# The second layer's modulation vectors are computed in the first layer's output projection and token choice, not with the filters

## The chip, the core and the metric

The kernel runs on one core of a Trainium2 chip. TensorE (PE) multiplies, VectorE (DVE), ScalarE (ACT) and GpSimd (POOL) work on the results, and SyncE (SP) issues most of the DMA transfers. Each engine takes its instructions in a fixed order, decided when the program is built, and an instruction that waits holds all that stand behind it on that engine. The metric is the device time of one execution in microseconds (us); less is better.

## The reference

Two layers work on 1024 latent tokens and 256 context tokens of width 1024. In each layer a modulation of six rows for the latent and six for the context tokens shifts, scales and gates the stream:

```python
mod_l = (jax.nn.silu(c) @ p['mod_w'] + p['mod_b'])[:, None, :]      # mod_w: 1024 x 6144, per layer
mod_c = jax.nn.silu(c_ctx) @ p['mod_w'] + p['mod_b']
hl = modulate(rmsnorm(xl, p['norm1_g']), sh1_l, sc1_l)
ul = hl @ p['w_in']
xl = xl + g1_l * token_mixers(ul, p, cos, sin, keys_l)              # attention, convolution, Hyena; then w_out
hl2 = modulate(rmsnorm(xl, p['norm2_g']), sh2_l, sc2_l)
xl = xl + g2_l * expert_choice_ffn(hl2, p)                          # 16 experts each choose 128 tokens
```

The Hyena part needs long filters that depend on the weights alone. The modulation depends on the two conditioning vectors alone, so the second layer's six rows can be made at any time before that layer starts.

## The kernel before

The program runs through `consts`, `filters` (both layers' Hyena filters and modulation), and then for each layer `win` (first norm and input projection), `mla` (attention, with the convolution and Hyena work beside it), `wout` (output projection, gated residual, router scores, choice of tokens) and `moe` (the experts). A scheduler merges the work of neighbouring stages into one order per engine when the program is built.

**Modulation.** `mod(l, ...)` takes two of the six rows at a time. For each pair it makes eight steps. A step loads 128 x 2048 floats of `mod_w` (1 MB) into a tile `mw`, of which there are three, and multiplies it with the two conditioning vectors `cT`, padded to 32 columns. Four matmuls of 512 columns go to four groups of 32 partitions of one PSUM bank, `macc`. After eight steps DVE adds the bias tile `mb`, scales where a gain `mg` belongs, and SP stores the rows to the DRAM tensor `modd`. The bias loads are issued on ACT's queue. `filters` chains `mod(0)` and `mod(1)` into one list of steps, `steps`, and takes one with `feed(1)` after each piece of filter work.

**Filters.** `spectra` multiplies filter taps (`dh`, `dl`: two parts of each number) with tables `fw` that POOL loads, three matmuls for each product (L95, L96, L97), into banks `p`. DVE and POOL scale the result `gg`, and SP stores it to `gd` or `gdc`.

**Output projection.** In `wout`, `channels(i)` and `heads(i)` handle a tile of 128 tokens: matmuls into banks `mm`, the residual into `xres`, four transposes into each of two banks `tp`, router scores into banks `rt`. `order` lists the ten tiles; tile 7 is the last. Then `route` chooses the tokens: short DVE operations on a tile `ro` with a few small matmuls between them.

**Experts.** `moe` starts with loads of expert 0's weights (four tiles `raw` of 2 MB), and with the matmuls `dt<-rhs,ohc` and `dt<-rhs,oh` that turn the choice into row numbers, by which tokens are gathered.

Of the kernel before, what the change touches and what calls it, by code (L numbers as in the profile page):

```python
# [14 lines left out]
F32 = mybir.dt.float32  # L15
# [4 lines left out]
ALU = mybir.AluOpType  # L20
# [9 lines left out]
def _bc(ap, n):  # L30

    return bass.AP(tensor=ap.tensor, offset=ap.offset, ap=[[0, n]] + [list(x) for x in ap.ap])
# [19 lines left out]
class Kernel:  # L52
# [81 lines left out]
    def mod(self, l, P, ps):  # L134

        nc, A, V = self.nc, self.A, self.V
        w_ = A["mod_w"][l].rearrange("(p k) n -> p k n", k=8)
        for v in range(0, 6, 2):
            acc = ps("macc")
            b = self.t(P, [128, 512], F32, "mb", bufs=1)  # L140
            g = self.t(P, [128, 512], F32, "mg", bufs=1)
# [8 lines left out]
            for k in range(8):  # L150
                w = self.t(P, [128, 2048], F32, "mw", bufs=3)
# [10 lines left out]
                nc.sync.dma_start(self.modd[l][v + j // 2][:, 512 * (j % 2):512 * (j % 2) + 512], b[32 * j:32 * j + 2, :])  # L162
            yield
        self.dump(f"mod{l}", self.modd[l])


    def sin(self, P, out, x, n):
# [180 lines left out]
    def filters(self):  # L348
        A = self.A
        with ExitStack() as es:  # L350
            M = self.pool(es, "mod", 2)
            F = {"f": self.pool(es, "taps", 1), "p": self.pool(es, "sums", 1)}
            ps = self.banks(es, macc=2, p=6)
            steps = chain(self.mod(0, M, ps), self.mod(1, M, ps))

            def feed(n):
                for _ in range(n):
# [10 lines left out]
            with ExitStack() as es2:  # L368
                PL = self.pool(es2, "mlp", 1)
                with ExitStack() as es3:  # L370
                    P = self.pool(es3, "mlps", 1, side="right")
# [669 lines left out]
    def wout(self, l, R):  # L1041
# [4 lines left out]
        with ExitStack() as es:  # L1046
# [6 lines left out]
            else:  # L1053
                PW = self.pool(es, f"wow{l}", 1)
                P = self.pool(es, f"woy{l}", 2)
                PX = self.pool(es, f"wox{l}", 2, side="right")
            ps = self.banks(es, tp=2, mm=4, rt=1, st=1) if last else self.banks(es, tp=2, mm=4, rt=1, st=1)
            gn = self.t(R["pool"], [128, 8], F32, "gn", bufs=1)
            nc.sync.dma_start(gn, A["gn_cols"][l])
            rw = self.t(R["pool"], [128, 8, 32], F32, "rw", bufs=1)  # L1060
# [124 lines left out]
            def router():  # L1185

                n = 1 if last else 2
                rr = self.t(PX, [128, 8, 16], F32, "rr", bufs=1)
                rc = self.t(PX, [128, 2, 2, 8], F32, "rc", bufs=1)
                rs = self.t(PX, [128, 32], F32, "rsum", bufs=1)  # L1190
                nc.sync.dma_start(rr, A["router_w"][l])
                nc.sync.dma_start(sel, A["k_sel"])
                for j, v in enumerate((4, 3)):
                    for s in range(n):
                        nc.sync.dma_start(rc[:, j, s], self.modd[l][v, s].rearrange("(k p) -> p k", p=128))
                if last:
                    G.memset(rw, 0.0)
                    G.memset(rs, 0.0)
                for s in range(n):
                    e = slice(16 * s, 16 * s + 16)  # L1200
                    G.tensor_tensor(rw[:, :, e], rr, rc[:, 0, s].unsqueeze(2).to_broadcast([128, 8, 16]), ALU.mult)
                    tmp = self.t(PX, [128, 8, 16], F32, "rtmp", bufs=1)
                    G.tensor_tensor(tmp, rr, rc[:, 1, s].unsqueeze(2).to_broadcast([128, 8, 16]), ALU.mult)
                    V.tensor_reduce(rs[:, e], tmp.rearrange("p k e -> p e k"), AX.X, ALU.add)
                p = ps("rt")
                self.mm(p[:, 0:32], self.ones[:, 0:1].to_broadcast([128, 128]), rs)
                V.tensor_copy(cst, p[:, 0:32])
# [15 lines left out]
            for n, i in enumerate(order):  # L1223
                end = heads(i)
                if i == 7:
                    self.route(R, ps, "mm" if last else "tp", row() if last else self.t(PX, [128, 1024], F32, "ro", bufs=1))
                    end()
                if n + 2 < nt:
                    channels(order[n + 2])
                if i == 9:  # L1230
                    ar, wk = (self.t(PX, [16, 256], F32, n, bufs=1) for n in ("arc", "wkc"))
                    self.route_ctx(R, ps, ar, wk)
# [595 lines left out]
```

## Time and profile before

| | |
|---|---|
| runs | 3397.47 us median of 3 (3392.35 to 3399.98) |
| profiled execution | 3397.73 us, span 3395.9 us from the first to the last instruction |
| TensorE matmul busy | 3123.1 us, 92% of the span |
| VectorE busy | 2531.3 us, 75% |
| ScalarE busy | 1690.2 us, 50% |
| DMA moved | 660.84 MB, mean 195 GB/s |
| mean granted TensorE clock | 0.954 of full speed |

The busy shares are means over stages with different limits. The span holds the filters up to about 248 us, the first layer's output projection from about 966 us, its choice of tokens up to about 1147 us, and its experts after that. Times in the rows below are microseconds from the start of the span.

### The profile page before, as it was taken

The numbers are of one execution on the slowest core, as the hardware profiler recorded it, in microseconds if no ns is written. First come the engines' busy times: TensorE is split into PE (matmuls) and PEld (weight loads), VectorE is DVE, ScalarE is ACT, GpSimd is POOL, SyncE is SP. The second block draws the span as 40 slices with busy tenths as digits, with TensorE's granted clock in tenths as the row PEclk, the third lists the DMA queues.
The fourth block names the chain that finished last, engine by engine and source line by source line (L and its number), as shares of the span: only waits on it lengthen the run. The fifth ranks groups of instructions, "written<-read, shape, count | busy, mean of one in ns | idle before, by whom it ended". The sixth has DMA issues, their size and how long they took to land. (4 is left out here: it accounts for less than half of the span.)

```text
span 3395.9 us, 42767 instructions
## 1 busy us (share of the span) xinstructions
PE 3123.1 (92%) x15607; PEld 2226.8 (66%) x15607; DVE 2531.3 (75%) x3520; ACT 1690.2 (50%) x2447; POOL 1295.2 (38%) x1128
## 2 busy tenths in 40 slices
PE   8898989999999599999999969899998959999996
PEld 2467865666567376666666657656664747888885
DVE  7755698777657677777777656977775769998986
ACT  4315235433443256656565543353434427777775
POOL 4421255754653212112221122565557423433334
PEclk9898989999999799999999979899999969999998
DMA  8881112231253567777777631221233469999994
GB/s 306 323 279 53 38 64 82 54 104 43 73 162 116 209 241 289 278 286 279 290 292 274 225 101 44 81 72 51 69 110 99 149 235 347 378 382 372 382 378 176
DMA packets 142523, 660.84 MB, mean 195 GB/s; under 512 B 24712, under 2 KB 63272, under 8 KB 111593
## 3 DMA queue, kind: packets, MB, share of 16 engines
q1 hardware_dynamic: 117129, 582.89, 45.6%
q0 software_dynamic: 24768, 74.05, 7.9%
q8 instruction: 123, 2.02, 0.2%
q10 hardware_dynamic: 416, 1.18, 0.1%
q14 instruction: 87, 0.71, 0.1%
HBM read 589.28 MB, written 68.78 MB: 194 GB/s over the span
## 5 line engine op out<-in xcount | busy, mean ns | idle before, releaser
L91 DVE TENSOR_TENSOR mwl<-raw,mwh 128x1024 fp32r<-128x1024 f32 x710 | 881.5, 1278 | 217.5 <-ACT mwh L90 207.2
L90 ACT ACTIVATE mwh<-raw 128x1024 fp32r<-128x1024 f32 x768 | 791.8, 1057 | 350.5 <-PE acc L97 118.1
L96 PE MATMUL acc<-mwl,xh 128*128 128x512 f32 x1024 | 405.0, 396 | 0.0
L97 PE MATMUL acc<-mwh,xl 128*128 128x512 f32 x1024 | 403.0, 396 | 0.1
L95 PE MATMUL acc<-mwh,xh 128*128 128x512 f32 x1024 | 373.7, 401 | 6.0 <-ACT xh L90 6.0
L803 POOL TENSOR_TENSOR psum<-psum,pt 128x512 f32<-128x512 f32 x252 | 332.3, 1338 | 66.7 <-ACT pt L788 56.8
L788 ACT ACTIVATE pt<-s 128x512 f32<-128x512 f32 (+1 forms) x336 | 195.9, 586 | 257.4 <-PE s L97 220.8
L1528 POOL DMA_INDIRECT xd<-ymoe,idx x31 | 113.4, 3656 | 541.6 <-DVE ymoe L1524 465.1
L758 DVE TENSOR_REDUCE mx<-p 128x1 f32<-128x512 f32 (+1 forms) x374 | 206.0, 585 | 70.0 <-PE p L100 68.9
L95 PEld LDWEIGHTS acc<-mwh,xh 128*128 128x128 f32 x1024 | 192.4, 189 | 68.6 <-ACT mwh L90 10.9
L96 PEld LDWEIGHTS acc<-mwl,xh 128*128 128x128 f32 x1024 | 193.9, 189 | 40.1 <-DVE mwl L91 0.8
L91 POOL TENSOR_TENSOR mwl<-raw,mwh 128x1024 fp32r<-128x1024 f32 x58 | 150.1, 2592 | 181.3 <-ACT mwh L90 117.5
L97 PEld LDWEIGHTS acc<-mwh,xl 128*128 128x128 f32 x1024 | 192.8, 189 | 39.1 <-DVE xl L91 0.6
L100 PE MATMUL o<-pt,Vt 128*64 128x512 f32 (+1 forms) x672 | 184.7, 613 | 0.0
L564 DVE SCALAR_TENSOR_TENSOR cacc<-pad,cw,cacc 128x1295 f32<-128x1295 f32 (+1 forms) x90 | 165.8, 1842 | 1.3
L97 PE MATMUL mm<-hTh,wfl 128*128 128x512 f32 (+1 forms) x400 | 151.3, 379 | 12.8 <-DVE wfl L91 12.8
L95 PE MATMUL mm<-hTh,wfh 128*128 128x512 f32 (+1 forms) x400 | 152.5, 381 | 4.0 <-ACT wfh L90 4.0
L96 PE MATMUL mm<-hTl,wfh 128*128 128x512 f32 (+1 forms) x400 | 152.0, 380 | 0.0
L562 POOL TENSOR_TENSOR cacc<-cacc,tap 128x1295 f32<-128x1295 f32 (+1 forms) x30 | 97.0, 3233 | 120.7 <-ACT tap L561 118.5
L100 PE MATMUL cx<-raw,xcT 128*32 128x512 f32 x1024 | 123.7, 607 | 0.0
L95 PE MATMUL mm<-woh,yhh 128*128 128x512 f32 x280 | 115.7, 416 | 8.5 <-ACT wt L1129 4.4
L96 PE MATMUL mm<-wol,yhh 128*128 128x512 f32 x280 | 111.9, 400 | 0.1
(546 smaller groups left out, 7228.9 us busy)
## 6 DMA issues: line engine op xcount, KB each, us to landing
raw<-in_w_gate_dram SPq DMA_DIRECT2D x64, 2048.0 KB
raw<-in_w_up_dram SPq DMA_DIRECT2D x64, 2048.0 KB
raw<-in_w_down_dram SPq DMA_DIRECT2D x64, 2048.0 KB
mw<-in_mod_w_dram SPq DMA_DIRECT2D x48, 1024.0 KB
ht<-in_k_C_dram POOLq DMA_DIRECT2D x24, 512.0 KB, 5.1
wfr<-in_w_fm_dram SPq DMA_DIRECT2D x20, 512.0 KB
hd<-h SPq DMA_DIRECT2D x18, 512.0 KB
fw<-in_k_filt_dram POOLq DMA_DIRECT2D x17, 512.0 KB, 5.8
```

Of the source, the lines that this page charges most:

```text
L90: self.S.activation(hi, src, AF.Copy)
L91: (eng or self.V).tensor_tensor(lo, src, hi.bitcast(F32), ALU.subtract)
L95: mm(out, ah, bh, start=first, stop=False, skip_group_check=True)
L96: mm(out, ah, bl, start=False, stop=False, skip_group_check=True)
L97: return mm(out, al, bh, start=False, stop=last, skip_group_check=True)
L100: return self.T.matmul(out, a, b, start=first, stop=last, skip_group_check=True)
L562: G.tensor_tensor(a, a, t, ALU.add)
L564: V.scalar_tensor_tensor(a, x, w2[:, ct, k:k + 1], a, ALU.mult, ALU.add)
L758: V.tensor_reduce(mx[:, q, n:n + 1], p[:, :N], AX.X, ALU.max)
L788: S.activation(pt[:, :N], p[:, :N], AF.Exp, scale=ATT_SCALE)
L803: (V if tail and n > 8 else G).tensor_tensor(sm[:, :N], st.sums[i][:, :N], pt[:, :N], ALU.add)
L1528: G.indirect_dma_start(self.xd[l], bass.IndirectOffsetOnAxis(ap=d["idx"], axis=0), y, None, compute_op=ALU.add)
```

## The change

`filters` keeps only `mod(0)`. A new function, `mod_row`, makes the second layer's modulation in `wout` of the first layer, one row at a time: six rows of eight steps, 48 steps, each with a load of 128 x 1024 floats (512 KB) into the one tile `mw` and four matmuls of 256 columns. There is one `mb`, one `mg` and one bank `macc`; for that bank `tp` goes from two to one. Four steps are asked for after each tile of tokens, and all that are left after tile 7, behind the choice. The bias and gain loads move from ACT's queue to SP's. `rr` and `rtmp` take the place of the tile `lpart`. The second layer's `wout` makes no steps.

```diff
--- before.py
+++ after.py
@@ -162,6 +162,33 @@
                 nc.sync.dma_start(self.modd[l][v + j // 2][:, 512 * (j % 2):512 * (j % 2) + 512], b[32 * j:32 * j + 2, :])
             yield
         self.dump(f"mod{l}", self.modd[l])
+
+    def mod_row(self, l, P, ps):
+
+        nc, A, V = self.nc, self.A, self.V
+        w_ = A["mod_w"][l].rearrange("(p k) n -> p k n", k=8)
+        for v in range(6):
+            acc = ps("macc")
+            b = self.t(P, [128, 256], F32, "mb", bufs=1)
+            V.memset(b, 0.0)
+            for j in range(4):
+                nc.sync.dma_start(b[32 * j:32 * j + 2, :], _bc(A["mod_b"][l, v * 1024 + 256 * j:v * 1024 + 256 * j + 256], 2))
+            if v in (1, 4):
+                g = self.t(P, [128, 256], F32, "mg", bufs=1)
+                V.memset(g, 0.0)
+                for j in range(4):
+                    nc.sync.dma_start(g[32 * j:32 * j + 2, :], _bc(A["norm1_g" if v == 1 else "norm2_g"][l, 256 * j:256 * j + 256], 2))
+            for k in range(8):
+                w = self.t(P, [128, 1024], F32, "mw", bufs=1)
+                nc.sync.dma_start(w, w_[:, k, v * 1024:v * 1024 + 1024])
+                for j in range(4):
+                    self.mm(acc[32 * j:32 * j + 32, :256], self.cT[:, k, :], w[:, 256 * j:256 * j + 256], k == 0, k == 7)
+                yield
+            V.tensor_tensor(b, acc[:, :256], b, ALU.add)
+            if v in (1, 4):
+                V.scalar_tensor_tensor(b, b, 1.0, g, ALU.add, ALU.mult)
+            for j in range(4):
+                nc.sync.dma_start(self.modd[l][v][:, 256 * j:256 * j + 256], b[32 * j:32 * j + 2, :])
 
 
     def sin(self, P, out, x, n):
@@ -351,7 +378,7 @@
             M = self.pool(es, "mod", 2)
             F = {"f": self.pool(es, "taps", 1), "p": self.pool(es, "sums", 1)}
             ps = self.banks(es, macc=2, p=6)
-            steps = chain(self.mod(0, M, ps), self.mod(1, M, ps))
+            steps = self.mod(0, M, ps)
 
             def feed(n):
                 for _ in range(n):
@@ -1054,7 +1081,13 @@
                 PW = self.pool(es, f"wow{l}", 1)
                 P = self.pool(es, f"woy{l}", 2)
                 PX = self.pool(es, f"wox{l}", 2, side="right")
-            ps = self.banks(es, tp=2, mm=4, rt=1, st=1) if last else self.banks(es, tp=2, mm=4, rt=1, st=1)
+            ps = self.banks(es, tp=2, mm=4, rt=1, st=1) if last else self.banks(es, tp=1, mm=4, rt=1, st=1, macc=1)
+
+            steps = iter(()) if last else self.mod_row(1, self.pool(es, f"mod{l}", 1), ps)
+
+            def feed(n):
+                for _ in range(n):
+                    next(steps, None)
             gn = self.t(R["pool"], [128, 8], F32, "gn", bufs=1)
             nc.sync.dma_start(gn, A["gn_cols"][l])
             rw = self.t(R["pool"], [128, 8, 32], F32, "rw", bufs=1)
@@ -1185,7 +1218,7 @@
             def router():
 
                 n = 1 if last else 2
-                rr = self.t(PX, [128, 8, 16], F32, "rr", bufs=1)
+                rr = self.t(PX, [128, 128], F32, "lpart").rearrange("p (k e) -> p k e", k=8)
                 rc = self.t(PX, [128, 2, 2, 8], F32, "rc", bufs=1)
                 rs = self.t(PX, [128, 32], F32, "rsum", bufs=1)
                 nc.sync.dma_start(rr, A["router_w"][l])
@@ -1199,7 +1232,7 @@
                 for s in range(n):
                     e = slice(16 * s, 16 * s + 16)
                     G.tensor_tensor(rw[:, :, e], rr, rc[:, 0, s].unsqueeze(2).to_broadcast([128, 8, 16]), ALU.mult)
-                    tmp = self.t(PX, [128, 8, 16], F32, "rtmp", bufs=1)
+                    tmp = self.t(PX, [128, 128], F32, "lpart").rearrange("p (k e) -> p k e", k=8)
                     G.tensor_tensor(tmp, rr, rc[:, 1, s].unsqueeze(2).to_broadcast([128, 8, 16]), ALU.mult)
                     V.tensor_reduce(rs[:, e], tmp.rearrange("p k e -> p e k"), AX.X, ALU.add)
                 p = ps("rt")
@@ -1227,6 +1260,10 @@
                     end()
                 if n + 2 < nt:
                     channels(order[n + 2])
+                feed(4)
+                if i == 7:
+                    for _ in steps:
+                        pass
                 if i == 9:
                     ar, wk = (self.t(PX, [16, 256], F32, n, bufs=1) for n in ("arc", "wkc"))
                     self.route_ctx(R, ps, ar, wk)
```

**On TensorE, in the filters.** Before, these rows stood where the second layer's steps begin; `p` products of the filters stand between steps of the modulation.

```order
L100 MATMUL macc_661<-mw_715,cT_71 32x512 [waits DMAHW0_49]
...
L100 MATMUL macc_661<-mw_736,cT_71 32x512 [waits DMAHW7_49]
...
L100 MATMUL macc_661<-mw_756,cT_71 32x512 [waits DMAHW1_49]
...
L100 MATMUL macc_661<-mw_778,cT_71 32x512 [waits DMAHW3_49]
...
L95 MATMUL p_888<-dh_237_848,fw_871 128x512 [waits Activation_49]
L96 MATMUL p_888<-dl_238_849,fw_871 128x512 [waits DVE_49]
L97 MATMUL p_888<-dh_237_848,fw_871 128x512
L95 MATMUL p_888<-dh_237_848,fw_871 128x512 [waits Activation_49]
L96 MATMUL p_888<-dl_238_849,fw_871 128x512 [waits DVE_49]
L97 MATMUL p_888<-dh_237_848,fw_871 128x512
L100 MATMUL macc_661<-mw_798,cT_71 32x512 [waits DMAHW1_49]
...
L95 MATMUL p_888<-dh_237_848,fw_871 128x512 [waits Activation_49]
```

Of the change, the same products (`p_823` now) stand without them:

```order
L97 MATMUL p_808<-dh_215_751,fw_806 128x512
L95 MATMUL p_823<-dh_226_783,fw_806 128x512 [waits Activation_49]
L96 MATMUL p_823<-dl_227_784,fw_806 128x512 [waits DVE_49]
L97 MATMUL p_823<-dh_226_783,fw_806 128x512
L95 MATMUL p_823<-dh_226_783,fw_806 128x512 [waits Activation_49]
L100 MATMUL p_808<-exh_221_770,er_781 128x512 [waits DMASW2_49]
L100 MATMUL p_808<-exl_222_771,er_781 128x512
L96 MATMUL p_823<-dl_227_784,fw_806 128x512 [waits DVE_49]
L97 MATMUL p_823<-dh_226_783,fw_806 128x512
```

All 24 steps of the second layer, of four matmuls each, are gone from the filters; the rest keeps its order.

**On TensorE, around the choice of tokens.** Before, from the transpose of the affinities (`tp` with `aff`) to the experts' first matmul:

```order
L1299 MATMUL tp_9558<-ident_60,aff_8090 128x128 [waits DVE_49]
L100 MATMUL tp_9637<-ro_9550,ident_60 16x128 [waits DVE_49]
L100 MATMUL tp_9641<-ro_9550,rows_same_8093 128x1 [waits DVE_49]
L100 MATMUL tp_9648<-ro_9550,rows_same_8093 128x1 [waits DVE_49,PE_49]
L100 MATMUL tp_9648<-ro_9550,rows_before_8095 128x1 [waits DVE_49]
...
L1345 MATMUL tp_9663<-ident_60,ro_9550 128x128 [waits DVE_49]
L100 MATMUL dt_9700<-rhs_8092,ohc_9701 64x4 [waits DVE_49,Pool_49]
...
L1430 MATMUL dt_9717<-ident_60,xgc_9714 128x32 [waits DMASW4_49]
```

Of the change, from the same transpose to the same matmul (`dt`), with the last rows in front of it:

```order
L1336 MATMUL tp_9653<-ident_60,aff_7898 128x128 [waits DVE_49]
L100 MATMUL macc_8914<-mw_8939,cT_71 32x256 [waits DMAHW4_49]
...
L100 MATMUL tp_9732<-ro_9645,ident_60 16x128 [waits DVE_49]
L100 MATMUL tp_9736<-ro_9645,rows_same_7901 128x1 [waits DVE_49,PE_49]
...
L100 MATMUL macc_8914<-mw_9066,cT_71 32x256 [waits DMAHW0_49]
...
L1382 MATMUL tp_9758<-ident_60,ro_9645 128x128 [waits DVE_49]
L100 MATMUL macc_8914<-mw_9072,cT_71 32x256 [waits DMAHW1_49]
...
L100 MATMUL macc_8914<-mw_9078,cT_71 32x256 [waits DMAHW2_49]
...
L100 MATMUL macc_9800<-mw_9843,cT_71 32x256 [waits DMAHW2_49]
...
L100 MATMUL macc_9800<-mw_9849,cT_71 32x256 [waits DMAHW3_49]
...
L100 MATMUL dt_9886<-rhs_7900,ohc_9887 64x4 [waits DVE_49,Pool_49]
...
L1467 MATMUL dt_9903<-ident_60,xgc_9900 128x32 [waits DMASW4_49]
```

Two steps now stand within the choice, and 27 behind its last transpose (`tp_9758`) and ahead of the experts' first matmul. The other 19 stand further up, the first in the attention and 18 between the output projection's products, about 30 rows apart.

**On SP, at the same place.** Before, the experts' first weights, the last stores of the residual and the normed tokens, and the next weights:

```order
L1151 DMA xd_19_87<-xres_9402 128x1024 [waits DMAHW4_49,DVE_49]
L1443 DMA raw_9692<-in_w_gate_dram 128x4096 [waits PE_49]
L1443 DMA raw_9694<-in_w_up_dram 128x4096 [waits DMAHW5_49,PE_49]
L1443 DMA raw_9696<-in_w_gate_dram 128x4096
L1443 DMA raw_9698<-in_w_up_dram 128x4096 [waits DMAHW7_49]
L1151 DMA xd_19_87<-xres_9482 128x1024 [waits DMAHW0_49,DVE_49]
L1183 DMA hd_22_90<-h_2131_9437 128x1024 [waits DMAHW1_49,DVE_49,Activation_49]
L1183 DMA hd_22_90<-h_2146_9517 128x1024 [waits DMAHW2_49,DVE_49,Activation_49]
L1594 DMA g2l_9872<-modd_6_74 128x1024 [waits DMAHW3_49]
```

Of the change:

```order
L183 DMA mw_8933<-in_mod_w_dram 128x1024 [waits DMAHW6_49,DMAHW4_49,PE_49]
L1480 DMA raw_9878<-in_w_gate_dram 128x4096 [waits DMAHW7_49]
L1480 DMA raw_9880<-in_w_up_dram 128x4096 [waits DMAHW0_49,PE_49]
L1480 DMA raw_9882<-in_w_gate_dram 128x4096 [waits DMAHW1_49]
L1480 DMA raw_9884<-in_w_up_dram 128x4096 [waits DMAHW2_49]
L1184 DMA xd_19_87<-xres_9577 128x1024 [waits DMAHW3_49,DVE_49]
L183 DMA mw_8939<-in_mod_w_dram 128x1024 [waits DMAHW6_49,PE_49]
L1216 DMA hd_22_90<-h_2139_9490 128x1024 [waits DMAHW5_49,DVE_49,Activation_49]
...
L183 DMA mw_9066<-in_mod_w_dram 128x1024 [waits DMAHW4_49,DMAHW0_49,PE_49]
L183 DMA mw_9072<-in_mod_w_dram 128x1024 [waits DMAHW1_49,DMAHW0_49,PE_49]
L183 DMA mw_9078<-in_mod_w_dram 128x1024 [waits DMAHW2_49,DMAHW1_49,PE_49]
...
L183 DMA mw_9279<-in_mod_w_dram 128x1024 [waits DMAHW3_49,PE_49]
```

Each load of `mw` waits for TensorE, that is for the step before it, which reads the same tile. The loads of the 27 last steps stand one behind the other, and the experts' next weights behind them.

## Rows read from the trace of the kernel before

**Rows 1.** Page, part 2: busy tenths of TensorE in 40 slices of 85 us.

```profile
PE   8898989999999599999999969899998959999996
```

**Rows 2.** Windows of 20 us: busy times by engine, PEclk, DMA share, GB/s.

```profile
100.00:120.00 20.00, 13.47 (x64) 4.45 (x63) 12.74 (x19) 6.48 (x11) 9.28 (x7) 0.76 0.78 296
120.00:140.00 20.00, 20.00 (x96) 12.00 (x95) 14.21 (x27) 4.66 (x9) 5.16 (x6) 0.87 0.91 331
...
160.00:180.00 20.00, 20.00 (x94) 12.91 (x93) 14.84 (x22) 4.77 (x8) 8.96 (x8) 1.00 0.88 306
```

**Rows 3.** Timeline of TensorE, 97 to 120 us: start, duration, what, idle before.

```profile
97.44 0.47 PE L95 MATMUL p<-dh,fw 128*128 128x512 f32 x1 [3.37 <-DMA fw<-in_k_filtc_dram]
...
104.45 2.78 PE L100 MATMUL macc<-mw,cT 128*32 128x512 f32 x24
112.15 1.94 PE L100 MATMUL macc<-mw,cT 128*32 128x512 f32 x8 [4.92 <-DMA mw<-in_mod_w_dram]
...
119.49 0.80 PE L95 MATMUL p<-dh,fw 128*128 128x512 f32 x1
```

**Rows 4.** Timelines of ACT and DVE: three waits for transfers.

```profile
112.72 1.15 ACT L90 ACTIVATE dh<-ff 128x512 fp32r<-128x512 f32 x2 [3.79 <-DMA mb<-in_mod_b_dram]
...
118.22 0.68 DVE L91 TENSOR_TENSOR exl<-fp,exh 1x512 fp32r<-1x512 f32 x1 [2.94 <-DMA gdc<-gg]
...
251.23 0.78 ACT L455 ACTIVATE hTh<-t,mcols 128x512 fp32r<-128x512 f32 x1 [29.08 <-DMA modd<-mb]
```

**Rows 5.** Timeline of TensorE, 240 to 249 us.

```profile
240.20 0.39 PE L96 MATMUL p<-dl,fw 128*128 128x512 f32 x1
240.42 0.40 PE L97 MATMUL p<-dh,fw 128*128 128x512 f32 x1
240.75 1.06 PE L100 MATMUL macc<-mw,cT 128*32 128x512 f32 x8
241.75 0.50 PE L95 MATMUL p<-dh,fw 128*128 128x512 f32 x1
...
248.46 1.15 PE L452 MATMUL t<-ident,xin 128*128 128x128 f32 x8
```

**Rows 6.** Window of 50 us in the output projection.

```profile
1000.00:1050.00 50.00, 50.00 (x289) 39.00 (x287) 39.51 (x64) 20.24 (x33) 20.60 (x28) 1.00 0.42 148
```

**Rows 7.** Timeline of TensorE in the choice of tokens.

```profile
1123.79 0.47 PE L1299 MATMUL tp<-ident,aff 128*128 128x128 f32 x1 [2.20 <-DVE aff L1250]
1138.87 0.60 PE L100 MATMUL tp<-ro,ident 32*16 32x128 f32 x2 [14.61 <-DVE ro L1296]
...
1143.06 0.99 PE L100 MATMUL tp<-ro,rows_before 128*128 128x1 f32 x4
1145.86 0.48 PE L1345 MATMUL tp<-ident,ro 128*128 128x128 f32 x1 [1.81 <-DVE ro L1343]
1147.08 0.34 PE L100 MATMUL dt<-rhs,ohc 128*64 128x4 f32 x2 [0.74 <-DVE ohc L1396]
```

**Rows 8.** Windows of 10 us in the choice of tokens.

```profile
1120.00:1130.00 10.00, 1.66 (x15) 0.78 (x7) 8.00 (x56) 5.99 (x7) 3.25 (x3) 0.50 0.98 372
1130.00:1140.00 10.00, 0.60 (x2) 0.12 (x2) 8.48 (x46) 0.00 (x0) 0.00 (x0) 0.50 0.51 207
```

**Rows 9.** Timeline of SP: last of expert 0's four weight loads.

```profile
1111.12 0.43 SPq L1443 DMA_DIRECT2D raw<-in_w_up_dram  x1
```

**Rows 10.** Timelines of SP and ACT: 512 KB issued by SP, ACT waits for it.

```profile
2018.93 0.80 SPq L440 DMA_DIRECT2D xin<-xc  x2
...
2022.40 1.06 ACT L444 ACTIVATE junk<-xin 128x1024 bf16<-128x1024 f32 x1 [2.33 <-DMA xin<-xc]
```

**Rows 11.** Timelines of TensorE and SP: a step, and the load that waits for its tile.

```profile
8.72 1.94 PE L100 MATMUL macc<-mw,cT 128*32 128x512 f32 x8
...
10.70 0.33 SPq L152 DMA_DIRECT2D mw<-in_mod_w_dram  x1
```

**Rows 12.** Page, part 6: POOL's 512 KB loads, last number us to landing.

```profile
ht<-in_k_C_dram POOLq DMA_DIRECT2D x24, 512.0 KB, 5.1
```

## Prediction

> **What bounds the kernel now.** I read the page first. TensorE is busy in nine tenths or more of most slices of 85 us, so what holds TensorE holds the kernel; of the low digits, the 5 in the 14th slice (1104 to 1189 us) is the choice of tokens in layer 1, and that is the stretch to look at [rows 1]. Then I looked at the two places that the change touches, the filters and the first layer's output projection with its choice, in windows and in each engine's order of time.
>
> In the filters the DMA engines are busy for 0.78 to 0.91 of the time, but from 120 us on TensorE is busy all the time too [rows 2]. Transfers alone set the pace only near 104 to 119 us: six steps of the second layer's modulation stand in TensorE's queue there, three of them run together at 104.45 and the other three each start late for their load [rows 3]. In the output projection TensorE has no gap (50.00 of 50 us) [rows 6]. In the choice it is the other way round: TensorE waits for DVE, at half the clock (PEclk 0.50), from the transpose at 1123.79 to the experts' first matmul at 1147.08 [rows 7, 8]. That is the empty room into which work could be put.
>
> **The change, part by part.** The sum is made against the profiled execution, 3397.73 us (1.8 us around its span of 3395.9), which stands 0.26 us above the median of the runs.
>
> *Taken out of the filters: 24 steps.* A step costs TensorE more than its busy time. Normal products start 0.22 us apart (240.20, 240.42); with a step between, the next one starts 1.33 us later (241.75), so a step holds the queue for 1.11 us [rows 5]. 18 of the 24 stand between products after 119.5 us: 18 x 1.11 = 20.0 us. The first six fill 104.45 to 119.49, 15.0 us [rows 3]. Not all of that comes back, since the products behind them need operands from ACT and DVE. What I take is the time those engines themselves stood behind the modulation's transfers: ACT 3.8 us behind a bias load, DVE 2.9 us behind a store that was queued with three 1 MB loads [rows 4], together 6.7 (ends 0 and 15.0). A table load that came 3.4 us late while these loads ran [rows 3] may come earlier: 2 (ends 0 and 3.4). The first write of `win` waits for the last store of these rows and starts at 251.23, while its transposes began at 248.46 [rows 4, 5]: 1 (ends 0 and 2). Sum: 20.0 + 6.7 + 2 + 1 = 29.7, say **30 us less**, ends 15 (if the tables become the limit) and 40. POOL's and SP's queues lose work here; nothing new waits.
>
> *Put between the output projection's products: 19 steps, 18 of them in this stage.* Half the columns: a step of 512 columns took 1.06 us at full clock and 1.94 us at half [rows 3, 5], that is 0.18 fixed and 0.88 that goes with columns and clock. 256 columns give 0.62 us at full and 1.06 at half clock. The queue is held for 1.11 - 0.44 = 0.67 us, x 19 = **12.5 us more**, bare, since TensorE has no gap there [rows 6]. Their loads have about 30 products, 30 x 0.23 = 7 us, to land, and need about 3.5 (below). But SP issues them in order behind stores that wait for DVE, and behind each stalled step all of TensorE's queue stands. Ends: 0, and 18 exposed loads, 63 us. The cover is twice what a load needs, so I stay near the lower end: **8 us more**. The one bank `tp` and the tile shared by `rr`, `rtmp` and `lpart` make small waits; the two steps just ahead of the choice follow each other after a few products only. Together **3 us more** (ends 1 and 5).
>
> *Within the choice: two steps.* The load of the first is issued behind the experts' four loads of 2 MB. The last of those is issued at 1111.12 [rows 9], and the transfers run until about 1135: 372 GB/s up to 1130 and 207 x 10 us after it, five more microseconds at that rate [rows 8]. So the row lands near 1136.5 and its step ends near 1137.6. TensorE is next wanted at 1138.87 [rows 7]. Cost 0, with 1.3 us to spare. If that cover is gone, each microsecond is one of the path. The second step fits between 1144.05 and 1145.86.
>
> *Behind the choice: 27 steps, one after the other.* This is the large term. The order has them between the choice's last transpose and the experts' first matmul. There is one `mw`, and each load waits for the step before. So a step is a closed round: TensorE's end to SP's issue, 0.04 us (8.72 + 1.94 = 10.66 to 10.70) [rows 11], say 0.06; issue to use of 512 KB, 2022.40 - 2018.93 = 3.47 us [rows 10], say 3.5, as the row pieces lie apart in memory; the product at half clock, 1.06 us. Sum 4.62 us. The first load goes out at about 1145.1, lands at 1148.6, and its step ends at 1149.7, 2.6 us after the experts' first matmul started before; 26 more: 26 x 4.62 = 120.1. Three times a new row begins, and four stores and four bias loads go ahead of a weight load on SP, mostly beside a load under way: 0.5 each, 1.5 (ends 0 and 10). **124 us more.** Nothing hides them: all that the experts need from TensorE stands behind. What DVE and ACT do next hangs on it, POOL's gathers need the row numbers, and the four `raw` tiles are full, so weights can't run ahead either. Bounds of the round: 0.04 + 3.47 + 0.62 = 4.13 (full clock), and 0.06 + 5.1 (a 512 KB load of POOL's) [rows 12] + 1.06 = 6.22; the term is then 110 or 174.
>
> The Trainium skill, "DMA: Bandwidth & Descriptors", section "Anatomy of one DMA", puts a transfer at 2.0 us fixed plus its bytes at 436 GB/s, which for 512 KB is an estimate of 3.2 us. The trace's 3.47 is 0.27 longer, with a second transfer behind it. By the page the 27 steps would cost 27 x 0.3 = 8 us less and the kernel would take 3507 us.
>
> **Sum.** 3397.7 - 30 + 12.5 + 8 + 3 + 124 = **3515 us**, 3.5% slower.
>
> **The rivals.**
>
> *A. The steps among the products stall.* Each waits out its load, because SP stands behind stores: 18 x 3.5 = 63 us in place of 8: 3570 us. For it: SP's loads of `mw` now share a queue with stores that wait for DVE. Against it: the cover of 7 us. It decides if SP is late by more than 3.5 us on most of them. Chance 0.10.
>
> *B. Transfers, not TensorE, bound the filters.* Then the saving is the second layer's 25.2 MB at about 311 GB/s [rows 2], 81 us instead of 30: 3464 us. For it: the DMA share of 0.9. Against it: TensorE's 20.00 of 20 us. Chance 0.08.
>
> *C. The experts' weights hold the choice.* If their loads start 10 us later against the transpose than before, the step within the choice is late by 10 - 1.3 = 8.7 us: 3524 us, inside the range. Chance 0.06.
>
> *D. The loads run ahead (the other side).* If the loads of the last 27 steps did not have to wait for the step before, their 14 MB could land beside the output projection, where the DMA share is 0.42 [rows 6], and the steps, 27 x 0.62 = 17 us, would fit in the choice, where TensorE is idle: 3397.7 - 30 + 23.5 = 3391 us, on the border between no change and faster; with the ends 40, 0 and 1 for the other terms, 3371. It decides at a round of (30 - 23.5) / 27 = 0.24 us, and at those ends 0.98. Against it: there is one `mw`, and each of these loads waits for TensorE in SP's order. Chance 0.03.
>
> **How the numbers follow.** The forecast as worked out has 0.73. Its own ends: 3397.7 - 40 + 12.5 + 1 + 110 = 3481, and 3397.7 - 15 + 12.5 + 40 + 5 + 174 = 3614, where the upper ones hardly come together. The range is 3475 to 3585: it takes in the forecast's lower end, A and C, and leaves out B, D and the top of the forecast and of A, about 2 in 10. A measurement of this kernel can tell about 0.2% (6.8 us) from no change. Only D comes that near; with a rest for what I don't see: faster 0.02, within 0.2% 0.02, slower 0.96.
>
> **What would show it.** The first transposes of `win` start near 218 us, not 248, and no step of 512 columns stands after 97 us. In the output projection TensorE stays without long gaps. Behind the transpose of `ro` come 27 equal rounds of about 4.6 us, each with TensorE idle for some 3.5 us until the DMA of `mw`, at PEclk 0.50; the experts' first matmul comes about 125 us after that transpose, not 1.2 us after it. The forecast is wrong if the rounds are shorter or overlap, if TensorE waits for `mw` between the products too, or if `win` starts much earlier or no earlier.

## The result, and the profile after

The changed kernel takes **3524.95 us** (median of 5 runs, 3514.7 to 3531.93), the kernel before, run beside it, 3395.57 us (5 runs, 3392.35 to 3399.98): ratio **1.0373**, 95% interval 1.0356 to 1.039. The forecast was 3515 us, the range 3475 to 3585. The profiled execution took 3524.95 us, its span is 3523.1 us, 127.2 more than before.

The page first: busy tenths of TensorE, and PEclk, the clock granted to it in tenths of full speed, in 40 slices of 88 us. Where [rows 1] has one 5, the 13th to 15th slices (1057 to 1321 us) now have 7, 2 and 5, the 2 at half the clock.

```profile
PE   8888989999997259999999978989999969999996
PEclk9899999999998569999999988999999979999998
```

These are the choice of tokens and what now stands behind it. The timeline of TensorE there answers to [rows 7]; 27 steps lie between the transpose at 1140.36 and the experts' first matmul (`dt`).

```profile
1118.29 0.48 PE L1336 MATMUL tp<-ident,aff 128*128 128x128 f32 x1 [2.20 <-DVE aff L1287]
1132.26 1.08 PE L100 MATMUL macc<-mw,cT 128*32 128x256 f32 x8 [13.50 <-DMA mw<-in_mod_w_dram]
1133.37 0.60 PE L100 MATMUL tp<-ro,ident 32*16 32x128 f32 x2
...
1138.48 1.08 PE L100 MATMUL macc<-mw,cT 128*32 128x256 f32 x8
1140.36 0.47 PE L1382 MATMUL tp<-ident,ro 128*128 128x128 f32 x1 [0.80 <-DVE ro L1380]
1143.24 1.08 PE L100 MATMUL macc<-mw,cT 128*32 128x256 f32 x8 [2.40 <-DMA mw<-in_mod_w_dram]
1147.83 1.08 PE L100 MATMUL macc<-mw,cT 128*32 128x256 f32 x8 [3.51 <-DMA mw<-in_mod_w_dram]
...
1162.84 1.08 PE L100 MATMUL macc<-mw,cT 128*32 128x256 f32 x8 [4.46 <-DMA mw<-in_mod_w_dram]
...
1262.53 1.08 PE L100 MATMUL macc<-mw,cT 128*32 128x256 f32 x8 [3.65 <-DMA mw<-in_mod_w_dram]
1267.25 1.08 PE L100 MATMUL macc<-mw,cT 128*32 128x256 f32 x8 [3.64 <-DMA mw<-in_mod_w_dram]
1269.24 0.34 PE L100 MATMUL dt<-rhs,ohc 128*64 128x4 f32 x2 [0.91 <-DVE ohc L1433]
```

There is one wait for one load in each round: 4.59 us from 1143.24 to 1147.83, 4.72 from 1262.53 to 1267.25, and a longer one (1162.84) where a new row's stores and bias loads go ahead on SP. In a window of the same stretch (columns as in [rows 2]: window, its length, busy us of PE, of its weight loads, of DVE, ACT and POOL, then PEclk, DMA share, GB/s) TensorE is busy for a fifth of the time, and the DMA engines move 109 GB/s against 372 in [rows 8]: neither is full.

```profile
1150.00:1200.00 50.00, 10.82 (x80) 2.07 (x80) 1.39 (x4) 0.00 (x0) 0.00 (x0) 0.50 0.38 109
```

In the filters no step stands behind 96 us any more, but TensorE now waits there for others. First its timeline, then its waits from 96 to 231 us (total, times, longest):

```profile
99.53 0.40 PE L97 MATMUL p<-dh,fw 128*128 128x512 f32 x1
108.16 0.79 PE L95 MATMUL p<-dh,fw 128*128 128x512 f32 x1 [8.24 <-ACT dh L90]
...
231.28 1.05 PE L479 MATMUL t<-ident,xin 128*128 128x128 f32 x8
```

```profile
PE p L95 <- DMA fw<-in_k_filt_dram: 8.8, 6, 2.1
PE p L95 <- ACT dh L90: 8.2, 1, 8.2
PE p L96 <- DVE dl L91: 2.4, 2, 2.0
```

During the long wait for `dh` its granted clock fell to 0.50 (from 104 us on). The first row is the 17 us behind that product, the second the 17 us behind the same product before the change, where it started at 119.49 [rows 3]:

```profile
108.16:125.16 17.00, 14.96 (x40) 10.50 (x41) 12.29 (x23) 5.61 (x10) 5.92 (x8) 0.50 0.11 32
119.49:136.49 17.00, 17.00 (x81) 9.88 (x78) 14.00 (x27) 4.91 (x8) 4.55 (x5) 0.83 0.93 345
```

In the output projection a step among products, and the wait for `mw` there, 960 to 1130 us, without the one in the choice:

```profile
996.66 0.39 PE L96 MATMUL mm<-wol,yhh 128*128 128x512 f32 x1
996.98 0.64 PE L100 MATMUL macc<-mw,cT 128*32 128x256 f32 x8
997.55 0.50 PE L97 MATMUL mm<-woh,yll 128*128 128x512 f32 x1
```

```profile
PE macc L100 <- DMA mw<-in_mod_w_dram: 0.7, 1, 0.7
```

Start times of the same instructions before and after place the 127.2 us:

| place | before | after | shift | this stage |
|---|---|---|---|---|
| first transpose of `win` [rows 5] | 248.46 | 231.28 | -17.2 | filters -17.2 |
| transpose of `aff`, choice begins [rows 7] | 1123.79 | 1118.29 | -5.5 | output projection +11.7 |
| transpose of `ro`, choice ends | 1145.86 | 1140.36 | -5.5 | choice 0.0 |
| experts' first matmul | 1147.08 | 1269.24 | +122.2 | 27 steps +127.7 |
| end of the span | 3395.9 | 3523.1 | +127.2 | rest of the experts, and second layer +5.0 |

### The profile page after: what moved, and what is told of

Same layout as the page of the kernel before. It is cut to its first block, busy times and chain, and to the rows that moved or that the text cites. A ratio compares the mean times of both kernels' runs of the same rounds, so it can differ in the third digit from the quotient of the medians.

```text
span 3523.1 us, 43233 instructions
## 1 busy us (share of the span) xinstructions
PE 3142.4 (89%) x15799; PEld 2233.6 (63%) x15799; DVE 2532.8 (72%) x3525; ACT 1689.9 (48%) x2447; POOL 1288.3 (37%) x1128
## 3 DMA queue, kind: packets, MB, share of 16 engines
q10 hardware_dynamic: 352, 1.11, 0.1%
## 5 line engine op out<-in xcount | busy, mean ns | idle before, releaser
L90 ACT ACTIVATE mwh<-raw 128x1024 fp32r<-128x1024 f32 x768 | 791.6, 1057 | 345.2 <-PE acc L97 117.4
L100 PE MATMUL macc<-mw,cT 128*32 128x256 f32 (+1 forms) x576 | 73.0, 590 | 121.1 <-DMA mw<-in_mod_w_dram 121.1
L1446 POOL DMA_INDIRECT xgc<-hd,idc x16 | 29.1, 1821 | 299.4 <-DVE glc L1442 150.4
```

What stands on the lines that cost most here:

```text
L90: self.S.activation(hi, src, AF.Copy)
L100: return self.T.matmul(out, a, b, start=first, stop=last, skip_group_check=True)
```

## The experiments

Each was profiled, and timed against the kernel before on the same chip; ratios are to that, with 95% intervals. Diffs are against the changed kernel unless it is said otherwise. The first four ask what the steps cost in the filters, the next four what the steps cost behind the choice and among products, the last two whether a share of them pays.

**no_second_mod**

```diff
-            steps = iter(()) if last else self.mod_row(1, self.pool(es, f"mod{l}", 1), ps)
+            steps = iter(())
-        self.modd = [self.t(d, [6, 2, 1024], F32, f"modd{l}") for l in range(2)]
+        self.modd = [self.t(d, [6, 2, 1024], F32, "modd0")] * 2
```

> The changed kernel with the second layer's modulation left out everywhere (the second layer works with the first layer's modulation rows); the one bank for transposes, the bank for the modulation and the shared small tile stay. Theory 1, from the trace after: the filters give back 17 us (the first product of win's transposes starts 17.2 us earlier than before) and not 30, because TensorE then waits for tables and operands; the 128 us behind the choice and the 11 us in the output projection vanish: 3395.6 - 17 = 3379 us (3374 to 3384), 145 us faster than the changed kernel. Theory 2, the prediction's term: 30 us come back: 3366 us. Theory 3, rival B: transfers bound the filters, 81 us come back: 3315 us.

Measured: 3384.91 us, ratio 0.9958 (0.9944 to 0.9971), 14 us faster than before, where theory 1 had 17. The first transpose of `win` comes at 233.73, 14.7 us earlier, and `dt` 1.21 us behind the last transpose of the choice:

```profile
233.73 1.05 PE L479 MATMUL t<-ident,xin 128*128 128x128 f32 x8
...
1130.47 0.47 PE L1382 MATMUL tp<-ident,ro 128*128 128x128 f32 x1 [1.81 <-DVE ro L1380]
1131.68 0.34 PE L100 MATMUL dt<-rhs,ohc 128*64 128x4 f32 x2 [0.74 <-DVE ohc L1433]
```

So all of the second layer's modulation costs the kernel before 10 to 19 us (14.3 by the ratio, 13.7 by the medians), and the changed one some 140. The prediction's 30 us (3366) lie outside the interval, rival B's 81 us far outside.

**steps_no_loads** and **loads_no_steps** (both against the kernel before)

```diff
-                w = self.t(P, [128, 2048], F32, "mw", bufs=3)
-                nc.sync.dma_start(w, w_[:, k, v * 1024:v * 1024 + 2048])
+                if l == 0:
+                    w = self.held = self.t(P, [128, 2048], F32, "mw", bufs=3)
+                    nc.sync.dma_start(w, w_[:, k, v * 1024:v * 1024 + 2048])
+                else:
+                    w = self.held
```

```diff
-                        self.mm(acc[32 * j:32 * j + 32, :], self.cT[:, k, :], w[:, 512 * j:512 * j + 512], k == 0, k == 7)
+                        if l == 0 or k == 0:
+                            self.mm(acc[32 * j:32 * j + 32, :], self.cT[:, k, :], w[:, 512 * j:512 * j + 512], k == 0, l == 1 or k == 7)
+                        elif j == 0:
+                            self.mm(acc[0:32, 0:4], self.cT[:, k, :], w[:, 0:4], True, True)
```

> The kernel before, with the second layer's 24 steps of modulation kept in the filters at their places, but all of them reading the last weight tile of the first layer: their 24 loads of 1 MB are left out (the second layer's modulation is made of wrong weights). Theory 1: about 10 of the 17 us belong to the first six steps, which stand in TensorE's queue while their loads are late, and to the loads that stand beside the tables; without loads 3385 us (3382 to 3388). Theory 2: what the steps cost is TensorE's queue alone, and the loads are hidden: 3395 us, no change. Theory 3: it is the loads alone: all 17 us come back, 3379 us.

> The kernel before, with the second layer's 24 loads of 1 MB kept, but 21 of the 24 steps cut to one product of 4 columns (the second layer's modulation is not computed). Theory 1: the first six still wait for their loads, the 18 others give back TensorE's time only as far as tables and operands allow, some 6 us: 3389 us (3386 to 3392). Theory 2, TensorE's queue alone: all 17 us come back, 3379 us. Theory 3, the loads alone: 3395 us, no change.

Measured: without loads 3396.53 us, ratio 0.9988 (0.9976 to 1.0); without steps 3403.49 us, ratio 1.0012 (1.0002 to 1.0022). No theory had the second: with TensorE's work gone and the loads kept, `win` starts at 255.28, 6.8 us later than before; without the loads at 242.30, 6.2 us earlier, of which 2 us are left in the total (0 to 8 by the interval). The waits of TensorE without steps, 96 to 256 us:

```profile
PE macc L100 <- DMA mw<-in_mod_w_dram: 16.1, 6, 8.7
PE p L95 <- DMA fw<-in_k_filt_dram: 14.3, 6, 5.2
```

The work that TensorE got rid of came back as waits for transfers, of `mw` and of the tables `fw` alike: the shortened steps stand where they stood, and hold TensorE's queue until their loads land. At this place the loads alone give back 6.2 us and the work alone nothing; both together give 15 to 17 us.

**late_second_mod** (against the kernel before)

```diff
-            steps = chain(self.mod(0, M, ps), self.mod(1, M, ps))
+            steps = chain(self.mod(0, M, ps), [None] * 9, self.mod(1, M, ps))
...
             for _ in both:
-                feed(1)
+                feed(2)
```

> The kernel before with its whole computation; the second layer's modulation starts nine calls later, so that none of its steps stands between the tables of the second filter, and is fed two at a time in the later loop. Theory 1: the six steps in the stretch from 104 to 119 us cost about 10 us because TensorE's queue waits for their loads while the products behind them could run; moved to where TensorE waits for tables anyway they cost little: 3387 us (3383 to 3391). Theory 2: the steps cost their time in the queue wherever they stand: 3395 us, no change; the loads packed closer could also make it slower, 3400 us.

Measured: 3414.8 us, ratio 1.0046 (1.0032 to 1.006), slower than theory 1 (3387) and theory 2 (3395, or 3400 with the loads packed) had it. The product that stood at 119.49 came at 109.06, so the stretch up to there gave back its 10 us. But the same steps and loads packed into less time cost more than that later: `win` starts at 266.84, 18.4 us later. From 160 to 200 us, where before TensorE was busy for 39.48 of 40 us, the window reads (columns as in [rows 2])

```profile
160.00:200.00 40.00, 35.87 (x178) 21.73 (x176) 22.33 (x35) 6.12 (x10) 13.35 (x13) 0.96 0.89 309
```

From 96 us to `win` TensorE waits 6.8 us for DVE's `gg`, which it did not before. DVE in turn waits 43.4 us for the stores of `gg` (33.9 before), and on SP these share a queue with the loads of `mw`, which wait 51.4 us for TensorE to free a tile (36.8 before). Whether the transfers or the order of SP's queue cost more was not separated.

**two_mw**

```diff
-                    self.route(R, ps, "mm" if last else "tp", row() if last else self.t(PX, [128, 1024], F32, "ro", bufs=1))
+                    self.route(R, ps, "mm" if last else "tp", row())
-                w = self.t(P, [128, 1024], F32, "mw", bufs=1)
+                w = self.t(P, [128, 1024], F32, "mw", bufs=2)
```

> The changed kernel, whole computation, with two tiles mw instead of one (room is made by putting ro into one of the three xres tiles). The order now has 34 steps among the output projection's products, 4 within the choice and 10 behind it. Theory 1, a closed round of latency: with two tiles two rounds of 4.7 us overlap, so the steps behind the choice follow each other at 2.4 us, 24 us in all instead of 128; 34 steps among products at 0.62 to 0.67 us make 22 us: 3397.7 - 17 + 22 + 24 + 4 (what the second layer lost in the trace after) = 3431 us (3420 to 3440). Theory 2, the loads behind the choice are limited by bytes per second (105 to 112 GB/s in the trace after), so two at a time are each twice as slow: the steps stay 4.7 us apart, 47 us: 3454 us. Theory 3: the 34 steps stand in the queue until their loads land, 3.5 us each: over 3500 us.

Measured: **3429.5 us**, ratio 1.0083 (1.0066 to 1.01), where theory 1 said 3431: 29 us above the kernel before in place of 129. Of the 10 steps behind the choice, four from TensorE's timeline:

```profile
1163.88 1.08 PE L100 MATMUL macc<-mw,cT 128*32 128x256 f32 x8 [1.34 <-DMA mw<-in_mod_w_dram]
1166.38 1.08 PE L100 MATMUL macc<-mw,cT 128*32 128x256 f32 x8 [1.42 <-DMA mw<-in_mod_w_dram]
1169.20 1.08 PE L100 MATMUL macc<-mw,cT 128*32 128x256 f32 x8 [1.73 <-DMA mw<-in_mod_w_dram]
1171.94 1.08 PE L100 MATMUL macc<-mw,cT 128*32 128x256 f32 x8 [1.67 <-DMA mw<-in_mod_w_dram]
```

The mean distance is 2.69 us (1163.88 to 1171.94), where it was 4.7: two loads do overlap, and the rate of the transfers was not the limit. From the choice's last transpose (1147.74) to `dt` (1176.50) it is 28.8 us, where theory 1 had 24 for the 10 steps.

**half_bytes**

```diff
-                nc.sync.dma_start(w, w_[:, k, v * 1024:v * 1024 + 1024])
+                nc.sync.dma_start(w[:, 0:512], w_[:, k, v * 1024:v * 1024 + 512])
-                    self.mm(acc[32 * j:32 * j + 32, :256], self.cT[:, k, :], w[:, 256 * j:256 * j + 256], k == 0, k == 7)
+                    self.mm(acc[32 * j:32 * j + 32, :256], self.cT[:, k, :], w[:, 256 * (j % 2):256 * (j % 2) + 256], k == 0, k == 7)
```

> The changed kernel with half of the second layer's modulation weights left out: each step loads 256 KB instead of 512 and multiplies the same 512 columns twice; the products are as many and as long. 24 steps stand behind the choice, 21 among products. Theory 1, the wait of 3.6 us is a fixed part and a transfer at the rate of busy DMA engines (311 to 372 GB/s), so half the bytes take 0.75 us less: rounds of 3.95 us, 24 of them 95 us: 3397.7 - 17 + 13 + 95 + 4 = 3493 us (3483 to 3503). Theory 2, the wait goes with the bytes: rounds of 2.9 us, 70 us: 3468 us. Theory 3, the wait is fixed: rounds of 4.7 us, 113 us: 3511 us.

Measured: 3490.78 us, ratio 1.0254 (1.0237 to 1.0271); theory 1 had 3493. Two of the 24 steps, 3.82 us apart where 3.95 were expected:

```profile
1230.15 1.08 PE L100 MATMUL macc<-mw,cT 128*32 128x256 f32 x8 [2.74 <-DMA mw<-in_mod_w_dram]
1233.97 1.08 PE L100 MATMUL macc<-mw,cT 128*32 128x256 f32 x8 [2.74 <-DMA mw<-in_mod_w_dram]
```

TensorE's wait fell from 3.65 to 2.74 us, 0.91 for 256 KB less (in pieces half as long), so of the 3.65 about 1.8 go with the bytes and 1.8 do not. The Trainium skill, "DMA: Bandwidth & Descriptors", section "Anatomy of one DMA", has 2.0 us fixed and 436 GB/s, for transfers that GpSimd issues; these are SP's. The fixed part here is within 0.2 us of that, the part with the bytes is longer (256 KB in 0.91 us are 288 GB/s), and the estimate of 3.2 us that the prediction took from it was short of the 3.50 to 3.75 us of the rounds.

**two_halves**

```diff
-                w = self.t(P, [128, 1024], F32, "mw", bufs=1)
-                nc.sync.dma_start(w, w_[:, k, v * 1024:v * 1024 + 1024])
-                for j in range(4):
+                for h in range(2):
+                    w = self.t(P, [128, 512], F32, "mw", bufs=2)
+                    nc.sync.dma_start(w, w_[:, k, v * 1024 + 512 * h:v * 1024 + 512 * h + 512])
+                    for j in (2 * h, 2 * h + 1):
```

> The changed kernel, whole computation, with the one tile mw cut into two of 512 columns in the same room; each is loaded for itself (256 KB), so a step is two half steps. 24 steps (48 half steps) stand behind the choice, 22 among products. Theory 1, closed rounds of latency, two of them overlapping: a half load lands in about 2.9 us, a round is 0.06 + 2.9 + 0.54 = 3.5 us, and two half steps fit into each: 24 x 3.5 = 84 us: 3397.7 - 17 + 14 + 84 + 4 = 3483 us (3470 to 3495). Theory 2: the loads do not overlap, 7.0 us for a step, 168 us: 3567 us. Theory 3, the loads go by bytes per second alone: 4.7 us for a step, 113 us: 3512 us.

Measured: 3495.92 us, ratio 1.027 (1.0253 to 1.0288), 13 above theory 1. From the choice's last transpose (1153.33) to `dt` (1246.76) it is 93 us for 24 steps, 3.9 each where 3.5 were expected; the rest is ahead of the choice, where 22 steps in two pieces each cost 25.2 us (`win` at 230.56, 17.9 early; the transpose of `aff` at 1131.06, 7.3 late), 1.1 a step. TensorE waited there for `mw` only 2.1 us in all, and a half step among products holds its queue about as long as a whole one (996.07 to 996.95 is 0.88, less the 0.23 between two products 0.65): it is the number of pieces that costs, not the loads. It is 95 us above the kernel before in place of 129, with tiles that take the same room as the one.

**one_load**

```diff
-                w = self.t(P, [128, 1024], F32, "mw", bufs=1)
-                nc.sync.dma_start(w, w_[:, k, v * 1024:v * 1024 + 1024])
+                if v == k == 0:
+                    w = self.held = self.t(P, [128, 1024], F32, "mw", bufs=1)
+                    nc.sync.dma_start(w, w_[:, k, v * 1024:v * 1024 + 1024])
+                w = self.held
```

> The changed kernel with 47 of the second layer's 48 loads of modulation weights left out: all steps read the first tile of weights (the second layer's modulation is made of wrong weights). All 48 steps then stand among the output projection's products and none behind the choice. Theory 1: a step costs TensorE's queue 0.62 to 0.67 us wherever TensorE has no gap: 48 x 0.62 to 0.67 = 30 to 32 us, and nothing behind the choice: 3397.7 - 17 + 31 + 4 = 3416 us (3409 to 3420), still slower than the kernel before. Theory 2: the steps fill gaps in the output projection (its small products wait here and there for ACT and DVE): half of that, 3400 us. Theory 3: the 128 us are not the loads' but those of the steps or of the choice: over 3500 us.

Measured: 3404.67 us, ratio 1.001 (1.0 to 1.002), between theories 1 and 2. From `win` (230.65, 17.8 us early) to the transpose of `aff` (1126.99, 3.2 us late) the 48 steps cost 21.0 us, 0.44 each, less than the 0.66 that one holds the queue: some fill small waits of TensorE (5.2 us in all from 960 us to 1126, where the kernel before has 12.5 ahead of the transpose of `aff`). No step stands behind the choice, and there is no loss there:

```profile
1149.65 0.47 PE L1384 MATMUL tp<-ident,ro 128*128 128x128 f32 x1 [1.81 <-DVE ro L1382]
1150.86 0.34 PE L100 MATMUL dt<-rhs,ohc 128*64 128x4 f32 x2 [0.74 <-DVE ohc L1435]
```

**split_16** and **split_32** (two_mw, with the first `n` rows of the second layer kept in the filters: n = 4 and n = 2; the diff is that of n = 4)

```diff
-    def mod(self, l, P, ps):
+    def mod(self, l, P, ps, n=6):
-        for v in range(0, 6, 2):
+        for v in range(0, n, 2):
...
-        for v in range(6):
+        for v in range(4, 6):
...
-            steps = self.mod(0, M, ps)
+            steps = chain(self.mod(0, M, ps), self.mod(1, M, ps, 4))
```

> Whole computation: two thirds of the second layer's modulation (rows 0 to 3, 16 steps of 512 columns) stay in the filters at their places before, and the last two rows (16 steps of 256 columns, two tiles mw) are made in the output projection; none stands behind the choice. Theory 1, from the runs so far: the filters give back at most a third of 15 us, and the output projection pays 0.46 to 0.55 us a step as in the runs with one load and with two tiles, 8 us: 3395.6 - 5 + 8 = 3399 us, not to be told from the kernel before. Theory 2: in the filters the last steps cost most, since the tables wait for their loads there: 10 us come back, 3394 us.

> Whole computation: the first two rows of the second layer's modulation (8 steps) stay in the filters, the other four (32 steps of 256 columns, two tiles mw) are made in the output projection; none stands behind the choice. Theory 1: two thirds of 15 us come back, 32 steps cost 0.46 to 0.62 us, 15 to 20 us: 3395.6 - 10 + 17 = 3403 us (3399 to 3407), slower by 0.2%. Theory 2: the first eight steps are those that cost in the filters (they stand in TensorE's queue ahead of the second filter's products), so little comes back: 3411 us. Theory 3: the stretch of tables behind 120 us is what the loads slow, nearly all comes back: 3397 us.

Measured: 3407.62 us, ratio 1.0029 (1.0018 to 1.004), and 3414.18 us, ratio 1.0052 (1.0036 to 1.0068): 8 and 15 us above the kernel before, where 3 and 7 were expected. In split_16 the filters gave back 4.3 us (`win` at 244.15), as theory 1 allows, and the 16 steps cost 13.8 up to the transpose of `aff` (1133.25, 9.5 us late), 0.86 each where 0.46 to 0.55 were expected; why they cost more than in one_load and two_mw was not found. The choice itself took 30.5 us (1133.25 to 1163.72) where it takes 22.07 in [rows 7]; the last section says why. Most of that comes back behind it, since the span ends 9.9 us later than before. In split_32 the filters gave back 9.9 us (`win` at 238.59), the 10 of theory 1, and the 32 steps cost 21.1 up to the transpose of `aff` (1135.04, 11.3 us late), 0.66 each; its choice took 30.5 us too.

## Why the prediction was right

**The large term** was right in its mechanism and its size. The round was put at 4.62 us and measured at 4.58 to 4.83 (mean 4.70), but for two where a row begins; TensorE's wait in it at 3.5 + 0.06, and measured at 3.50 to 3.75; the term at 124 us, and measured at 127.7. Of the 3.7 us more, 2.0 are the slightly longer rounds, and 0.9 is `dt`'s wait for DVE behind the last step, which the sum did not have. The 1.5 us for three new rows were 1.9 in two of them (waits of 4.46 and 4.67 us, some 0.8 and 1.0 more than the others); in the third the bias loads went out behind the weight load and cost nothing. two_mw (rounds overlap), half_bytes (half of the wait goes with the bytes, half does not) and one_load (without loads no step is left behind the choice) show that the closed round of one tile makes it, not TensorE's work and not the rate of the transfers.

**The choice** cost nothing, as forecast: 15.08 us from `aff` to the next transposes, before and after. But of the 1.3 us to spare nothing was left. The step ended at 1132.26 + 1.08 = 1133.34, and the transposes started at 1133.37 without a wait for DVE of their own; DVE's last operation ahead of them ended at 1133.31. The last of the experts' four loads was issued 11.2 us ahead of the transpose of `aff` (1107.08), where it was 12.7 before [rows 7, 9]: 1.5 us later, which used up the cover. Rival C, which needs 10, was not the case, but any further delay would have been one of the path.

**The output projection** was put at 12.5 + 8 + 3 = 23.5 us and cost 11.7. The bare price holds: 996.66 to 997.55 is 0.89, less the 0.23 between two products 0.66, forecast 0.67 (19 x 0.67 is 12.7, not 12.5). The 8 us of stalls were wrong: TensorE waited for `mw` 0.7 us in all. The steps lie 6 to 10 us apart, but for the last, 4.5 behind the one before, and SP issues most of the loads right behind the step that frees the tile (a step ends at 990.15, the load goes out at 990.22). Rival A is out by the same row. The 3 us for the one bank `tp` and the shared tile were not there either: no_second_mod has both, and from `win` (14.7 early) to the transpose of `aff` (1108.37, 15.4 early) it loses nothing.

**The filters** were put at 30 us and gave back 17.2. This is the step that failed: "18 x 1.11 = 20.0 us". The first six steps gave more than forecast: the product behind them came 11.3 us earlier (119.49 to 108.16), where 6.7 + 2 were expected. From that product to the first transpose of `win` it was 128.97 us and is 123.12, so the other 18 steps gave back 5.9 us and not 20.0. The term took TensorE's full windows [rows 2] for the only limit there. With the steps gone three things took their place, 12.7 of the 14.1 us that are missing:

- TensorE waits 8.8 us for the tables `fw` behind that product, where it waited 2.7. Before, POOL issued most of these loads after a wait for TensorE to free the tile; now six in a row, from 154 to 189 us, leave POOL straight behind its own work on `gg`, and four of the six waits end with the landing of such a load, 4.9 to 5.7 us after it was issued. The DMA engines are not full there (0.49 of the time from 160 to 180 us, 0.88 before). One of these loads (TensorE's wait for it ends at 173.83):

```profile
167.35 1.68 POOL L368 TENSOR_TENSOR gg<-gg,skip 128x512 f32<-128x512 f32 x1 [2.56 <-DVE gg L366]
168.97 0.56 POOL L342 DMA_DIRECT2D fw<-in_k_filt_dram  x1
```

- It waits 2.0 us for `dl`.
- It runs at the lower clock for longer. The 8.24 us in which it waits for `dh` were filled with steps before. Now the clock falls to 0.50 in them and stays there until 125 us, and products start 0.43 us apart (116.02, 116.45), not 0.23. By the two windows above (busy time times the share of the clock that was not granted) that is an estimate of 14.96 x 0.50 - 17.00 x 0.17 = 4.6 us.

The lower end, "15 (if the tables become the limit)", was nearly the case. loads_no_steps agrees: take TensorE's work alone away, and nothing comes back. Rival B has a part of the truth (loads alone away: 6 us at `win`), but not its 81 us.

The 13 us too much in the filters and the 12 too much in the output projection cancel in the sum by luck; the total was better than its parts. The top end of 3614 has 40 us for the stalls, where the term's own end is 63; nothing hangs on it. The 5.0 us at the end stand in no term. 4.7 of them come where the first layer's experts end and the second layer begins (the same instructions are 122.0 us late up to 1920 us of the trace before and 126.7 late at 2110). All ten kernels of the experiments lose 0.3 to 4.8 us at that place against the same trace, those with the steps at their old places too, so it need not be the change; the cause stays open.

No version that does the whole computation beats the kernel before. What could be won is bounded by no_second_mod, 14 us, and one_load, with nearly all transfers left out, already costs more than that among products.

## What to carry to other kernels

Work with a load of its own may be put into a gap only if the load is on its way before the gap begins: with one tile each step is a closed round of load and product, and its price is the load's wait, however little the engine does. Here a second tile took back 100 of 129 us. And where an engine is full, look at what stands close behind it before its busy time is counted as a saving, and at what its clock does in the gaps that are left. Take the work away alone and the load alone, since the two need not add up.

## What was not expected of the hardware

In split_16 DVE was slow in the choice. Of its timeline, two operations of 128 x 64 that take 0.22 us in the changed kernel, and below them POOL's in the same microseconds:

```profile
1139.03 2.26 DVE L1345 TENSOR_TENSOR xres<-xres 128x64 f32<-128x64 f32 x1
1141.21 2.37 DVE L1346 TENSOR_TENSOR xres<-xres 128x64 f32<-128x64 f32 x1
```

```profile
1134.24 13.86 POOL L91 TENSOR_TENSOR mwl<-raw,mwh 128x1024 fp32r<-128x1024 f32 x6
```

Before, POOL did one of these six (2.36 us) within the choice and five behind it. Here all six run in it, each 2.3 us, and four of DVE's operations with two inputs took 2.26 to 2.37 us instead of 0.22, about the length of one of POOL's: some 8.4 us more, which is what the choice lost; what POOL had done early came back behind it. DVE's operations with one input in the same microseconds kept their length (0.21 us). split_32 shows the same four (2.26 to 2.37 us, from 1140.82, under POOL's six). two_mw has the choice in the same tile `xres`, but none of the six within it; there no operation of the choice is slow, and it takes 22.1 us. That fits the Trainium skill, "SBUF — State Buffer", section "Who interferes with whom", by which a DVE instruction with two inputs in SBUF contends with a GpSimd instruction that reads SBUF. No edit touches POOL's work: the order came out so when the tiles changed. A change that only moves steps on TensorE can cost on DVE.

TensorE's granted clock was 0.50, its lower level, all through the 127 us of rounds, in which it was busy for a fifth to a quarter of the time (10.82 of 50 us, then 11.90 of 50), and came back in the experts (1.00 from 1300 us).
